# Feed-forward of block 1 by block matrices: seven block products in place of eight

## Chip, cores and metric

The kernel runs on one core of one Trainium2 chip. The metric is the device time of one execution in microseconds (us). The core has five engines that run their own programs in order and wait for each other by semaphores: TensorE (PE, the matmuls), VectorE (DVE), ScalarE (ACT), GpSimd (POOL) and SyncE (SP), which issues nearly all transfers (DMA) between memory and SBUF here. Matmul results land in PSUM.

## What is computed

Two transformer blocks run over 1024 tokens of width 1024, in fp32. Block 1 has a convolution branch, an attention branch, and a feed-forward part; block 2 has differential attention beside a short convolution, and a mixture of experts. The change concerns the feed-forward part of block 1 alone:

```python
D_FF = ((8 * D_MODEL // 3 + 255) // 256) * 256      # 2816
...
        x = x + merged @ w_out[l]
        h2 = rmsnorm(x, g_ffn[l])
        gu = h2 @ w_ffn_in[l]
        x = x + (jax.nn.silu(gu[..., :D_FF]) * gu[..., D_FF:]) @ w_ffn_out[l]
    return x
```

Block 2 begins with `modulate(rmsnorm_2(h, ...), sh1, sc1)`, where shift and scale come from `silu(c) @ w_ada`, a matrix of 1024 x 6144 that multiplies one row.

## The kernel before

Every fp32 operand of a product is split into a high part, rounded to the type that PE multiplies, and a low part, the rest: `split` (line 213) is one ACT operation (the cast) and one DVE operation (the difference). A product is then three: high by high, low by high, high by low (`mm3`, line 267); its matmuls have a 128x128 stationary block and a 128x512 moving one, and go into one PSUM bank of 128x512.

The tokens are two halves of 512. `b1_out` (line 732) multiplies by `w_out`, adds into the eight residual tiles `x1` (128 tokens x 1024) and, behind the last column block, calls `store` for each half. `store` calls `norm_T` (line 746): `row_inv` gives one over the root mean square per token (squares on ACT, a few small DVE steps), DVE scales copies `xn`, PE transposes them (`tpx`), and a split puts eight pairs of operands (128 channels x 512 tokens) into SBUF.

`ffn` (line 774) goes over 22 blocks `f` of 128 hidden channels. `gu(f)` loads and splits the gate and the up weights of the block (`w_gu`, 128x1024 each) and makes four products `pg`, `pu` (2 halves x gate and up, 24 matmuls each); ACT takes the silu, DVE multiplies by `pu` (line 792), and the result is split into operands. `down` (line 797) takes two blocks at a time, loads two blocks of `w_ffn_out`, and for each of 8 token tiles and 2 column halves makes a product `pd` of 6 matmuls (12 the last time), which DVE adds into `x1` (line 807). Between these blocks stand the steps of `ada` (line 835): it loads `w_ada` in 128x512 pieces, DVE multiplies each by a scalar per partition and sums up (lines 849 and 851), and PE sums over partitions with a matrix of ones (`pada`). `ada_end` (line 861) reads the result back, adds bias and gains. Behind the last `down` of each half, `b2_prep` (line 894) stores the residual to DRAM (`d_h`), normalises and transposes the half for block 2, whose first products are `pq` by `w2_k`.

The order of each engine's program is that of the code; tiles come from rotating pools (`bufs` tiles of a name), and a write to a reused tile waits for its last reader. SP issues loads in the order of the code too, which runs ahead of the products by what the pools hold. Here six rows of weights `wr` (128x1024) and four split ones fit, and PSUM has 3 banks for `mm` (`pg`, `pu`, `pw`), 2 for transposes and 3 for `pd`.

## Time and profile before

| what | value |
| --- | --- |
| time, median of 3 runs | 2835.47 us (2834.75 to 2836.74) |
| the profiled execution | 2836.5 us |
| its span in the trace | 2834.7 us, 1.8 us less |
| TensorE busy | 2704.4 us, 95% |
| VectorE busy | 2000.4 us, 71% |
| ScalarE busy | 1331.1 us, 47% |
| GpSimd busy | 187.3 us, 7% |
| mean granted TensorE clock | 0.98 |
| from the first `pg` to the first `pq` | 793.09 to 1529.91 us |

Durations come from one profiled execution. A busy share is a mean over the whole span, while each stage has its own limit, so the stretches are read one by one. An engine's idle time is put down to what released it ("<-ACT ych"). The duration of a matmul overlaps the next one's; the distance of their starts tells how fast they follow each other. The granted clock is TensorE's: 1.00 is 2.4 GHz, 0.50 is 1.2 GHz.

### The profile page before, as it was taken

Reading aid. Unit: us, or ns where it says so; the run is one execution under the profiler, and the core shown is the slowest. Engines: PE = TensorE matmul, PEld = TensorE weight load, DVE = VectorE, ACT = ScalarE, POOL = GpSimd, SP = SyncE. Lnnn points to the kernel's source line nnn. Section 1 sums busy time; section 2 is a strip of 40 time slices with the busy share of each in tenths; the row PEclk is TensorE's granted clock in tenths of the full one; section 3 lists DMA queues with packets and bytes.
Section 4 is the critical chain, followed back from the end, with each engine's and each line's share of the span. In section 5 each row is a group of like instructions: output and inputs, shape, how many; then the busy total and the mean of one; then the engine's idle time right before and its main releaser. Section 6 shows DMA issues by size and latency. Waiting matters only on the chain.

```text
span 2834.7 us, 39695 instructions
## 1 busy us (share of the span) xinstructions
PE 2704.4 (95%) x14546; PEld 2273.4 (80%) x14546; DVE 2000.4 (71%) x3679; ACT 1331.1 (47%) x2499; POOL 187.3 (7%) x273
## 2 busy tenths in 40 slices
PE   6999999989999999999999998999999599999995
PEld 5899777768988888888888987888887488888874
DVE  5998688745454665543326567898758799999987
ACT  4223467631131222111124455666433488888885
POOL 0000011000000000000000033100000100000101
PEclk9999999999999999999999999999999799999997
DMA  3124422054312343311113412221155899999986
GB/s 126 53 75 108 138 82 65 31 193 150 105 45 60 109 149 117 117 54 45 45 60 122 135 58 75 94 87 53 53 169 206 299 385 393 392 393 393 391 296 156
DMA packets 164594, 430.77 MB, mean 152 GB/s; under 512 B 36088, under 2 KB 47200, under 8 KB 164400
## 3 DMA queue, kind: packets, MB, share of 16 engines
q1 hardware_dynamic: 157328, 405.69, 40.3%
q0 software_dynamic: 7072, 22.55, 3.5%
q8 instruction: 114, 1.87, 0.3%
q14 instruction: 80, 0.66, 0.1%
HBM read 368.60 MB, written 59.57 MB: 151 GB/s over the span
## 4 chain that ended last, share of the span: by engine, by line
PE 87%; DVE 5%; DMA 3%; ACT 2%; issue 2%; POOL 0%; SPq 0%; POOLq 0%; ACTq 0%; DVEq 0%
PE pg L274 8%; PE pu L274 8%; PE pd L274 8%; PE pgate L274 7%; PE pw L274 6%; PE pnat L274 5%; PE pq L274 4%; PE pa L274 3%; PE po L1152 3%; PE peg L1508 2%; PE peu L1510 2%; PE peu L1509 2%; PE peg L1509 2%; PE peg L1510 2%; PE peu L1508 2%
## 5 line engine op out<-in xcount | busy, mean ns | idle before, releaser
L218 DVE TENSOR_TENSOR wl<-wr,wh 128x1024 fp32r<-128x1024 f32 (+1 forms) x248 | 298.8, 1226 | 186.7 <-ACT wh L217 184.7
L217 ACT CAST wh<-wr 128x1024 fp32r<-128x1024 f32 (+1 forms) x248 | 256.8, 1052 | 354.7 <-PE pd L274 159.7
L218 DVE TENSOR_TENSOR wl<-op,wh 128x1024 fp32r<-128x1024 f32 x285 | 334.5, 1220 | 17.7 <-ACT wh L217 15.9
L217 ACT CAST wh<-op 128x1024 fp32r<-128x1024 f32 x285 | 294.2, 1057 | 40.4 <-PE peg L1509 17.3
L274 PE MATMUL pd<-wh,op 128*128 128x512 f32 x704 | 187.6, 390 | 0.0
L274 PE MATMUL pgate<-op,wh 128*128 128x512 f32 x640 | 177.3, 406 | 3.8 <-ACT op L220 3.6
L807 DVE TENSOR_TENSOR x<-x,pd 128x512 f32<-128x512 f32 x160 | 108.3, 685 | 65.2 <-PE pd L274 65.1
L274 PEld LDWEIGHTS pd<-wh,op 128*128 128x128 f32 x704 | 131.8, 188 | 27.3 <-ACT wh L217 0.2
L369 DVE SCALAR_TENSOR_TENSOR c<-a,w_half,c 128x1019 f32<-128x1019 f32 (+28 forms) x120 | 148.0, 1263 | 0.4
L792 DVE TENSOR_TENSOR silu<-silu,pu 128x512 f32<-128x512 f32 x44 | 30.2, 687 | 159.5 <-PE pu L274 159.3
L274 PEld LDWEIGHTS pgate<-op,wh 128*128 128x128 f32 x640 | 118.4, 191 | 29.3 <-ACT op L220 8.2
L1131 ACT ACTIVATE ex<-ps,nmm 128x512 f32<-128x512 f32 (+1 forms) x192 | 116.9, 618 | 48.8 <-DVE nmm L1127 40.8
L274 PE MATMUL pq<-wh,op 128*128 128x256 f32 x768 | 114.8, 291 | 0.8 <-ACT wh L217 0.5
L851 DVE SCALAR_TENSOR_TENSOR acc<-wada,silu_c,acc 128x512 f32<-128x512 f32 x112 | 82.0, 749 | 41.5 <-DMA wada<-in_w_ada_dram 40.5
L1527 PE MATMUL ped<-wh,ehh 128*128 128x512 f32 x256 | 103.4, 404 | 7.2 <-ACT wh L217 7.2
L274 PE MATMUL pw<-wh,op 128*128 128x256 f32 (+1 forms) x640 | 109.2, 307 | 0.0
L274 PE MATMUL pd<-wl,op 128*128 128x512 f32 x352 | 106.6, 390 | 0.0
L274 PEld LDWEIGHTS pq<-wh,op 128*128 128x128 f32 x768 | 103.4, 196 | 3.8 <-ACT wh L217 1.4
L1508 PE MATMUL peg<-wh,xsh 128*128 128x512 f32 x256 | 101.7, 397 | 0.4 <-ACT xsh L217 0.3
L1510 PE MATMUL peg<-wl,xsh 128*128 128x512 f32 x256 | 101.0, 395 | 0.9 <-DVE wl L218 0.9
L1510 PE MATMUL peu<-wl,xsh 128*128 128x512 f32 x256 | 101.7, 397 | 0.0
L1529 PE MATMUL ped<-wl,ehh 128*128 128x512 f32 x256 | 99.5, 395 | 2.2 <-DVE wl L218 2.1
(469 smaller groups left out, 6570.9 us busy)
## 6 DMA issues: line engine op xcount, KB each, us to landing
op<-in_w_down_dram SPq DMA_DIRECT2D x96, 512.0 KB, 7.5
op<-in_w_up_dram SPq DMA_DIRECT2D x95, 512.0 KB, 6.3
op<-in_w_gate_dram SPq DMA_DIRECT2D x94, 512.0 KB
wada<-in_w_ada_dram SPq DMA_DIRECT2D x96, 256.0 KB, 2.7
wr<-in_w_gu_dram SPq DMA_DIRECT2D x44, 512.0 KB, 3.6
wr<-in_w_gate_dram SPq DMA_DIRECT2D x34, 512.0 KB
wr<-in_w_up_dram SPq DMA_DIRECT2D x33, 512.0 KB, 6.0
wr<-in_w_down_dram SPq DMA_DIRECT2D x32, 512.0 KB, 8.4
```

The costliest lines, as they stand in the source:

```text
L217: nc.scalar.copy(hi, src)
L218: nc.vector.tensor_sub(lo, src, hi.bitcast(F32))
L274: r = nc.tensor.matmul(ps, a[k], b[k], start=first and s == 0 and k == 0, stop=last and s == 2 and k == n - 1)
L369: nc.vector.scalar_tensor_tensor(c[:, s:], a[:, :S - s], wh[:, j * 31 + 30 - s:j * 31 + 31 - s], c[:, s:], op0=OP.mult, op1=OP.add)
L807: v.tensor_add(xs[tt][:, sl], xs[tt][:, sl], p)
L1131: nc.scalar.activation(ex[:, sl], p, AF.Exp, bias=nmm, accum_out=z[:, m * 3 + pi:m * 3 + pi + 1])
L1152: nc.tensor.matmul(po[:, :256], part[:, j * 128:(j + 1) * 128], V[j0 + j], start=j0 + j == 0 and part is ah, stop=j0 + j == 9 and part is al)
L1508: nc.tensor.matmul(p, xh[:, ks], wh[:, ws], start=k == 0, stop=False)
L1509: nc.tensor.matmul(p, xl[:, ks], wh[:, ws], start=False, stop=False)
L1510: nc.tensor.matmul(p, xh[:, ks], wl[:, ws], start=False, stop=k == KD - 1)
L1527: nc.tensor.matmul(pd[half], a[:, fs], wh[:, ws], start=f == 0, stop=False)
L1529: nc.tensor.matmul(pd[half], a[:, fs], wl[:, ws], start=False, stop=f == KD - 1)
```

## The change

The feed-forward's matrices are taken as 2 x 2 blocks, and a product of such matrices is made from seven products of sums and differences of blocks (Winograd's form) in place of eight.

**Up.** The normalised tokens' operand has the blocks half 0 and half 1 by channels 0 to 511 and 512 to 1023. `ffn_norm` stores the residual `x1` to DRAM (`d_x1`) and scales the tiles in place. For half 0 it transposes and splits into B[1] and B[2]; for half 1 `ffn_sums` transposes, scales on ACT, and makes the five operands B[6], B[5], B[7], B[3], B[4] from sums of both halves: 33 operations on DVE (13 sums, 20 differences of splits) and 11 on POOL (`t3`, `t2`). `ffn_up(j)` makes, for j = 0 to 10, seven products for gate and up (m = 0, 1) of 128x512 weight blocks: 7 x 2 x 12 matmuls into 6 PSUM banks. Weight sums `sc` (s1, s2) are made by DVE, `s3` and s4 by POOL; each weight or sum is split into one tile `ws` (of 7). DVE adds the products together from PSUM (`plus`), ACT and DVE gate them, and the seven combinations needed later are stored to DRAM as `d_a{j}`, five of them made by POOL. `ada` becomes a generator, of which two steps stand behind each product for j of 1 and more.

**Down.** After all of it, pools are closed and opened again, `x1` is loaded back from `d_x1`, `ada_end` runs, and `ffn_down` makes seven products, 3, 5, 4, 1, 7, 6, 2. Each has 11 steps: load `ar` (a stored combination) and one or two blocks `br` of `w_ffn_out` (128x512 each), combine these into `bc` (DVE, or POOL in products 7 and 6), split both, and 12 matmuls into four PSUM banks. Then the four banks are added to (or taken from) one or two quarters of `x1`. `b2_prep` runs for half 0 behind product 7, for half 1 behind product 2.

The diff, cut where `...` stands (among it the old body of `ffn`, which stands above):

```diff
--- before.py
+++ after.py
...
@@ -771,55 +772,208 @@
...
-    def ffn(self, xs, xh, xl, then):
+    def ffn_norm(self, xs, half, g):
+        grp = xs[4 * half:4 * half + 4]
+        for tt in range(4 * half, 4 * half + 4):
+            self.nc.sync.dma_start(self.d_x1[tt], xs[tt])
+        inv = self.row_inv(grp)
+        for i, t in enumerate(grp):
+            self.nc.vector.tensor_scalar(t, t, inv[:, i:i + 1], None, op0=OP.mult)
+        if half == 0:
+            hi, lo = self.ops(0)
+            self.to_T(grp, hi, lo, g)
+            self.B = {1: (hi[:4], lo[:4]), 2: (hi[4:], lo[4:])}
+        else:
+            self.ffn_sums(grp, g)
+    def ffn_sums(self, grp, g):
+        nc = self.nc
+        v = nc.vector
+        (b11h, b11l), (b21h, b21l) = self.B[1], self.B[2]
+        new = {n: [self.op(1) if n in (5, 6) else self.page_of(self.pt) for _ in range(4)] for n in (6, 5, 7, 3, 4)}
+        fs = []
+        for k in range(4):
+            f = self.pg(name="x1", pool=self.px)
+            for kk in range(2):
+                tp = self.tp(name="tpx")
+                for i, t in enumerate(grp):
+                    nc.tensor.transpose(tp[:, i * 128:(i + 1) * 128], t[:, (k + 4 * kk) * 128:(k + 4 * kk + 1) * 128], self.ident)
+                nc.scalar.activation(f[:, kk * 512:(kk + 1) * 512], tp, AF.Copy, scale=g[:, k + 4 * kk:k + 4 * kk + 1])
+            fa, fb = f[:, :512], f[:, 512:]
+            t3 = self.hp(name="t3")
+            (nc.gpsimd if k else v).tensor_sub(t3, fb, fa)
+            v.tensor_sub(fa, fa, b11l[k].bitcast(F32))
+            v.tensor_sub(fa, fa, b11h[k].bitcast(F32))
+            t2 = self.hp(name="t2")
+            v.tensor_sub(t2, fb, fa)
+            self.split(t2, *new[6][k])
+            self.split(t3, *new[7][k])
+            fs.append((fa, fb, t2))
+        for k in range(4):
+            self.split(fs[k][0], *new[5][k])
+            nc.gpsimd.tensor_sub(fs[k][2], b21h[k].bitcast(F32), fs[k][2])
+            nc.gpsimd.tensor_add(fs[k][2], fs[k][2], b21l[k].bitcast(F32))
+        for k in range(4):
+            self.split(fs[k][1], *new[3][k])
+        for k in range(4):
+            self.split(fs[k][2], *new[4][k])
+        for n, o in new.items():
+            self.B[n] = [hi for hi, lo in o], [lo for hi, lo in o]
...
+    def wsplit(self, src):
+        t = self.wp.tile([128, 1024], F32R, name="ws", tag="ws", bufs=self.ws)
+        self.split(src, t[:, :512], t[:, 512:])
+        return t
+    def wk(self, src):
+        t = self.wsplit(src)
+        return [t[:, k * 128:(k + 1) * 128] for k in range(4)], [t[:, 512 + k * 128:640 + k * 128] for k in range(4)]
+    def ffn_up(self, j, ada):
         nc = self.nc
         v = nc.vector
         A = self.A
...
+        B = self.B
+        f0, f1 = [], []
+        for fs, f in ((f0, 2 * j), (f1, 2 * j + 1)):
+            for m in range(2):
+                r = self.wp.tile([128, 1024], F32, name="wr", tag="wr", bufs=4)
+                nc.sync.dma_start(r, A["w_gu"][2 * f + m])
+                fs.append(r)
+        L, R = slice(0, 512), slice(512, 1024)
+        def product(n, w):
+            ps = [self.mm(name=f"p{m}") for m in range(2)]
+            for m in range(2):
+                self.mm3(ps[m], w(m), B[n])
+            ada(2)
+            return ps
+        def tiles():
+            return [self.hp(name=n) for n in ("hg", "hu")]
+        def plus(out, x, ps):
+            for m in range(2):
+                v.tensor_add(out[m], x[m], ps[m])
+        def gate(x):
+            nc.scalar.activation(x[0], x[0], AF.Silu)
+            v.tensor_mul(x[0], x[0], x[1])
+        p = product(1, lambda m: self.wk(f0[m][:, L]))
+        u = tiles()
+        for m in range(2):
+            nc.scalar.copy(u[m], p[m])
+        p = product(2, lambda m: self.wk(f0[m][:, R]))
+        c11 = tiles()
+        plus(c11, u, p)
+        gate(c11)
+        s1, s2, s3, s4 = [], [], [], []
+        for m in range(2):
+            t = self.hp(name="sc")
+            v.tensor_add(t, f1[m][:, L], f1[m][:, R])
+            s1.append(self.wk(t))
+            v.tensor_sub(t, t, f0[m][:, L])
+            s2.append(self.wk(t))
+            s4.append(t)
+        p = product(6, lambda m: s2[m])
+        plus(u, u, p)
+        for m in range(2):
+            t = self.hp(name="s3")
+            nc.gpsimd.tensor_sub(t, f0[m][:, L], f1[m][:, L])
+            s3.append(t)
+        p = product(7, lambda m: self.wk(s3[m]))
+        c21 = tiles()
+        plus(c21, u, p)
+        p = product(5, lambda m: s1[m])
+        c22 = tiles()
+        plus(c22, c21, p)
+        plus(u, u, p)
+        gate(c22)
+        for m in range(2):
+            nc.gpsimd.tensor_sub(s4[m], f0[m][:, R], s4[m])
+        p = product(3, lambda m: self.wk(s4[m]))
+        plus(u, u, p)
+        gate(u)
+        p = product(4, lambda m: self.wk(f1[m][:, R]))
+        plus(c21, c21, p)
+        gate(c21)
+        c11, c12, c21, c22 = c11[0], u[0], c21[0], c22[0]
+        a11, a21, a12, a22 = c11, c12, c21, c22
+        d = self.dram.tile([8, 128, 512], F32, name=f"d_a{j}")
+        self.d_a.append(d)
+        def out(n, t):
+            nc.sync.dma_start(d[n], t)
+        def both(n, op, x, y, dst=None):
+            t = self.hp(name="hc") if dst is None else dst
+            op(t, x, y)
+            out(n, t)
+        out(3, a11)
+        out(4, a22)
+        both(1, nc.gpsimd.tensor_add, a11, a22)
+        both(2, nc.gpsimd.tensor_add, a21, a22)
+        both(6, nc.gpsimd.tensor_sub, a21, a11, a21)
+        both(5, nc.gpsimd.tensor_add, a11, a12)
+        both(7, nc.gpsimd.tensor_sub, a12, a22, a12)
+    def ffn_down(self, xs, then):
+        nc = self.nc
+        v = nc.vector
+        W = self.A["w_ffn_out"]
+        L, R = slice(0, 512), slice(512, 1024)
+        add, sub = v.tensor_add, v.tensor_sub
+        for n, b, c in ((3, ((0, R), (1, R), sub), ((0, R, add), (1, R, add))),
+                        (5, ((1, R),), ((0, L, sub), (0, R, add))),
+                        (4, ((1, L), (0, L), sub), ((0, L, add), (1, L, add))),
+                        (1, ((0, L), (1, R), add), ((0, L, add), (1, R, add))),
+                        (7, ((1, L), (1, R), nc.gpsimd.tensor_add), ((0, L, add),)),
+                        (6, ((0, L), (0, R), nc.gpsimd.tensor_add), ((1, R, add),)),
+                        (2, ((0, L),), ((1, L, add), (1, R, sub)))):
+            ps = [self.mm(name="pd") for _ in range(4)]
+            for j in range(DFF // 256):
+                t = self.hp(name="ar")
+                nc.sync.dma_start(t, self.d_a[j][n])
+                x = self.wsplit(t)
+                r = []
+                for o, cols in b[:2]:
+                    t = self.hp(name="br", bufs=6)
+                    nc.sync.dma_start(t, W[2 * j + o][:, cols])
+                    r.append(t)
+                if len(b) == 3:
+                    t = self.hp(name="bc")
+                    b[2](t, r[0], r[1])
+                else:
+                    t = r[0]
+                y = self.wsplit(t)
+                for i in range(4):
+                    q = slice(i * 128, (i + 1) * 128), slice(512 + i * 128, 640 + i * 128)
+                    self.mm3(ps[i], ([x[:, q[0]]], [x[:, q[1]]]), ([y[:, L]], [y[:, R]]), first=j == 0, last=j == DFF // 256 - 1)
+            for i in range(4):
+                for h, cols, op in c:
+                    t = xs[4 * h + i]
+                    op(t[:, cols], t[:, cols], ps[i])
+            if n == 7:
+                then(0)
+        then(1)
     def ada_setup(self):
...
@@ -849,12 +1004,12 @@
                         v.tensor_scalar(acc, w, s, None, op0=OP.mult)
                     else:
                         v.scalar_tensor_tensor(acc, w, s, acc, op0=OP.mult, op1=OP.add)
+                    yield
             for (r, cc), acc in zip(outs, accs):
...
                 nc.sync.dma_start(self.d_mod[r:r + 1, half * 512:(half + 1) * 512], acc[0:1])
...
@@ -1620,36 +1775,54 @@
         gates.finish()
         p.release()
         self.weights(2, 4)
-        self.psum(3, 2, 3)
+        self.psum(6, 2, 0)
         p = self.phase("pD")
         mh, ml = self.b1_merge()
         p.release()
-        px = self.phase("px1")
+        self.pt = self.open("pT", "right")
+        self.px = self.phase("px1")
         xs = self.b1_load_x()
-        pt = self.open("pT", "right")
         p = self.phase("pE")
...
         g = self.cload("g_ffn", [128, KD])
-        xh, xl = [], []
...
-        self.b1_out(mh, ml, xs, store)
+        self.d_x1 = self.dram.tile([NT, 128, D], F32, name="d_x1")
+        self.b1_out(mh, ml, xs, lambda half: self.ffn_norm(xs, half, g))
+        p.release()
+        self.px.release()
+        self.wp.release()
+        self.wp = self.open("wp", "left")
+        self.ws = 7
+        self.d_a = []
+        p = self.phase("pU")
+        for n, k in (("acc", 2), ("wada", 2), ("hc", 2), ("s3", 2), ("hg", 5), ("sc", 2), ("hu", 4)):
+            for _ in range(k):
+                self.hp(name=n)
         self.ada_setup()
-        self.ffn(xs, xh, xl, lambda half: None if x2_only else self.b2_prep(xs, half))
...
+        ada = Paced(self.ada())
+        for j in range(DFF // 256):
+            self.ffn_up(j, ada if j else lambda n: None)
+        ada.finish()
         p.release()
-        pt.release()
+        self.pt.release()
+        self.wp.release()
+        self.wp = self.open("wp", "left")
+        self.ws = 8
+        px = self.phase("px2")
+        xs = []
+        for tt in range(NT):
+            t = self.pg(name="x1")
+            self.nc.sync.dma_start(t, self.d_x1[tt])
+            xs.append(t)
+        p = self.phase("pV")
+        self.ada_end()
+        self.ffn_down(xs, lambda half: self.b2_prep(xs, half))
+        p.release()
         px.release()
+        self.wp.release()
+        self.wp = None
+        self.weights(2, 4)
+        self.psum(3, 2, 3)
...
```

DVE's program at the start of the feed-forward, before. `xn` are scaled tokens of half 1, `op0` its operands; `silu` and `op1` are the first gate's result and operands:

```order
L757 TENSOR_SCALAR xn_8174<-x1_7028,inv_row_8090 128x256
L757 TENSOR_SCALAR xn_8176<-x1_7030,inv_row_8090 128x256
L221 SCALAR_TENSOR_TENSOR op0_8066<-tpx_8158,c_g_ffn_7040,op0_8066 128x512
L221 SCALAR_TENSOR_TENSOR op0_8067<-tpx_8165,c_g_ffn_7040,op0_8067 128x512
L757 TENSOR_SCALAR xn_8178<-x1_7032,inv_row_8090 128x256
L792 TENSOR_TENSOR silu_8265<-silu_8265,pu_8240 128x512
L221 SCALAR_TENSOR_TENSOR op0_8068<-tpx_8180,c_g_ffn_7040,op0_8068 128x512
L221 SCALAR_TENSOR_TENSOR op0_8069<-tpx_8187,c_g_ffn_7040,op0_8069 128x512
L218 TENSOR_TENSOR op1_8268<-silu_8265,op1_8268 128x512
```

And after, where `f0` and `op1` are low parts of the summed operands, `ones` belongs to `ada_setup`, and `ws` is a split weight of the first steps:

```order
L219 TENSOR_TENSOR op1_8084<-x1_8166,op1_8084 128x512
L219 TENSOR_TENSOR f0_8092<-x1_8166,f0_8092 128x512
L219 TENSOR_TENSOR f0_8093<-t2_8114,f0_8093 128x512
L219 TENSOR_TENSOR f0_8094<-t2_8137,f0_8094 128x512
L219 TENSOR_TENSOR f0_8095<-t2_8160,f0_8095 128x512
L219 TENSOR_TENSOR f0_8096<-t2_8183,f0_8096 128x512
L209 MEMSET ones_f_8255 128x128
L210 CAST ones_8254<-ones_f_8255 128x128
L219 TENSOR_TENSOR ws_8268<-wr_8258,ws_8268 128x512
L219 TENSOR_TENSOR ws_8283<-wr_8260,ws_8283 128x512
L219 TENSOR_TENSOR ws_8304<-wr_8258,ws_8304 128x512
```

The normalisation of half 1 stood among the first products' work; now all of the sums stand ahead of the first split weight.

SP's program at the border from the last gate and up to the last projection back, before (`wr` is a weight's tile), as far as the loads for block 2 and the first store of the residual:

```order
L233 DMA wr_12569<-in_w_gu_dram 128x1024
L233 DMA wr_12575<-in_w_gu_dram 128x1024
L233 DMA wr_12693<-in_w_ffn_out_dram 128x1024
L233 DMA wr_12699<-in_w_ffn_out_dram 128x1024
L233 DMA wr_12705<-in_w_ffn_out_dram 128x1024
L233 DMA wr_12711<-in_w_ffn_out_dram 128x1024
L233 DMA wr_13264<-in_w2_k_dram 128x1024
L233 DMA wr_13270<-in_w2_k_dram 128x1024
L901 DMA d_h_12829<-x1_7018 128x1024
L901 DMA d_h_12829<-x1_7020 128x1024
```

And after, from the last stores of the combinations on (`hg` and `hc` hold them; `modt` is the first load of `ada_end`, and seven more such small ones follow it, then the first `ar`):

```order
L920 DMA d_a10_11918<-hg_11674 128x512
L1815 DMA x1_11943<-d_x1_7044 128x1024
L1815 DMA x1_11945<-d_x1_7044 128x1024
L920 DMA d_a10_11918<-hc_11929 128x512
L920 DMA d_a10_11918<-hg_11806 128x512
L1815 DMA x1_11947<-d_x1_7044 128x1024
L1815 DMA x1_11949<-d_x1_7044 128x1024
L1815 DMA x1_11951<-d_x1_7044 128x1024
L1815 DMA x1_11953<-d_x1_7044 128x1024
L1815 DMA x1_11955<-d_x1_7044 128x1024
L1815 DMA x1_11957<-d_x1_7044 128x1024
L1025 DMA modt_11962<-d_mod_8253 64x128
```

Loads of `w_ffn_out` stood among those of `w_gu`; now the stores of the last step and the whole reload of `x1` come first.

SP's program at the end of the feed-forward, after, where before the two `w2_k` loads stood ahead of the first `d_h` store (the last rows of the fence of before):

```order
L954 DMA ar_14097<-d_a10_11918 128x512
L1056 DMA d_h_13426<-x1_11951 128x1024
L1056 DMA d_h_13426<-x1_11953 128x1024
L1056 DMA d_h_13426<-x1_11955 128x1024
L1056 DMA d_h_13426<-x1_11957 128x1024
L234 DMA wr_14304<-in_w2_k_dram 128x1024
L234 DMA wr_14310<-in_w2_k_dram 128x1024
L234 DMA wr_14438<-in_w2_q_dram 128x1024
```

The stores of half 1's residual now stand ahead of the first weights of block 2.

## Rows read from the trace of the kernel before

**Rows 1.** The page, part 1 (busy us, share, instructions) and part 4 (chain).

```profile
PE 2704.4 (95%) x14546; PEld 2273.4 (80%) x14546; DVE 2000.4 (71%) x3679; ACT 1331.1 (47%) x2499; POOL 187.3 (7%) x273
...
PE 87%; DVE 5%; DMA 3%; ACT 2%; issue 2%; POOL 0%; SPq 0%; POOLq 0%; ACTq 0%; DVEq 0%
```

**Rows 2.** Windows: length, busy us of PE, PEld, DVE, ACT, POOL; PE clock, DMA share, GB/s.

```profile
1000.00:1100.00 100.00, 100.00 (x442) 82.42 (x441) 60.50 (x86) 16.61 (x23) 0.00 (x0) 1.00 0.43 132
```

**Rows 3.** Timeline of PE: start us, us, line, operation, count [idle before]; three stretches.

```profile
792.13 1.12 PE L274 MATMUL pw<-wl,op 128*128 128x256 f32 x8
793.09 2.00 PE L274 MATMUL pg<-f,wh 128*128 128x512 f32 x8
...
1003.05 1.07 PE L274 MATMUL pd<-wh,op 128*128 128x512 f32 x4
1003.96 0.62 PE L274 MATMUL pd<-wl,op 128*128 128x512 f32 x2
1004.41 1.07 PE L274 MATMUL pd<-wh,op 128*128 128x512 f32 x4
...
1529.00 1.07 PE L274 MATMUL pd<-wl,op 128*128 128x512 f32 x4
1529.91 2.57 PE L274 MATMUL pq<-wh,op 128*128 128x256 f32 x19
```

**Rows 4.** Groups of PE's instructions, 740 to 1620 us: count | busy us, mean ns | idle.

```profile
L274 PE MATMUL pd<-wh,op 128*128 128x512 f32 x704 | 187.6, 390 | 0.0
L274 PE MATMUL pd<-wl,op 128*128 128x512 f32 x352 | 106.6, 390 | 0.0
```

**Rows 5.** Waits of DVE, 740 to 1620 us: us in total, times, longest.

```profile
DVE silu L792 <- PE pu L274: 159.3, 33, 8.3
...
DVE acc L851 <- DMA wada<-in_w_ada_dram: 37.6, 32, 3.6
```

**Rows 6.** Timeline of DVE: the norm of half 0, from last addition to reciprocal root.

```profile
777.31 0.42 DVE L741 TENSOR_TENSOR x<-x,pw 128x256 f32<-128x256 f32 x1 [2.46 <-PE pw L274]
...
781.17 0.16 DVE L263 SCALAR_TENSOR_TENSOR inv_row<-rs_t,rs_i 128x4 f32<-128x4 f32 x1
```

**Rows 7.** Timeline of DVE, and its group of in-place scalings (busy, mean ns | idle).

```profile
1000.38 1.28 DVE L807 TENSOR_TENSOR x<-x,pd 128x512 f32<-128x512 f32 x2
...
L322 DVE TENSOR_SCALAR x<-x,inv_row 128x1024 f32<-128x1024 f32 x8 | 5.5, 749 | 0.1
```

**Rows 8.** Timeline of DVE and POOL at three places of block 2.

```profile
1658.08 1.81 DVE L1142 SCALAR_TENSOR_TENSOR ex<-ex,cf,ex 128x512 f32<-128x512 f32 x3
...
1668.26 3.12 DVE L1142 SCALAR_TENSOR_TENSOR ex<-ex,cf,ex 128x512 f32<-128x512 f32 x3
1669.49 1.60 POOL L989 TENSOR_TENSOR fp<-fp,rot 128x512 f32<-128x512 f32 x1
...
1759.32 3.76 DVE L250 TENSOR_SCALAR rs_i<-ms 128x4 int32<-128x4 int32 x1
1759.33 2.51 POOL L988 TENSOR_TENSOR fp<-fp,rope 128x512 f32<-128x512 f32 x2
1761.80 1.25 POOL L989 TENSOR_TENSOR fp<-fp,rot 128x512 f32<-128x512 f32 x1
```

**Rows 9.** Timeline of PE where block 1 turns from gates to merging.

```profile
601.34 0.80 PE L274 MATMUL py<-ych,wh 128*128 128x512 f32 x1 [6.74 <-ACT ych L220]
```

**Rows 10.** Windows with the columns of rows 2: that border, and the experts' stage.

```profile
600.00:605.00 5.00, 2.15 (x4) 0.94 (x4) 3.14 (x5) 3.30 (x6) 0.00 (x0) 0.50 0.83 285
605.00:610.00 5.00, 4.68 (x14) 3.20 (x13) 3.87 (x6) 2.99 (x5) 0.00 (x0) 0.72 0.83 239
2430.00:2440.00 10.00, 10.00 (x52) 8.34 (x51) 10.00 (x11) 8.55 (x12) 0.56 (x1) 1.00 1.03 420
```

**Rows 11.** The page, part 6, with groups below it: DMA issues, KB, us to landing.

```profile
ta<-d_gate SPq DMA_DIRECT2D x16, 256.0 KB, 2.9
...
d_h<-x SPq DMA_DIRECT2D x8, 512.0 KB, 2.6
```

More of the change, by code (lines that the diff above doesn't have):

```diff
@@ L798, in down @@
-        def down(fs, last=False):
-            ws = [self.weight(A["w_ffn_out"][f]) for f in fs]
-            for tt in range(NT):
-                q = slice((tt % 4) * 128, (tt % 4 + 1) * 128)
-                for c in range(2):
-                    p = self.at(name="pd")
-                    sl = slice(c * 512, (c + 1) * 512)
-                    self.mm3(p, ([hs[f][0][tt // 4][:, q] for f in fs], [hs[f][1][tt // 4][:, q] for f in fs]),
-                             ([w[0][:, sl] for w in ws], [w[1][:, sl] for w in ws]))
-                    v.tensor_add(xs[tt][:, sl], xs[tt][:, sl], p)
-                if last and tt % 4 == 3:
-                    then(tt // 4)
-            for f in fs:
-                del hs[f]
@@ L832, in ada_setup, with ada @@
         self.ones = self.constr(1.0, "ones")
-    def ada(self, step):
+    def ada(self):
         nc = self.nc
         v = nc.vector
-        for half in range(2):
-            j = 2 * step + half
+        for j in range(12):
+            step, half = j // 2, j % 2
             outs = [(step, 0)] + ([(6 + step, 1)] if step < 2 else [])
@@ L1600, in moe, with block1 @@
             nc.gpsimd.indirect_dma_start(out=out, out_offset=at, in_=fr, in_offset=None)
[L1603 removed]
+    def block1(self):
         p = self.phase("pA")
```

56 lines of the change are left out of this document (10 added, 46 removed).

## The prediction

> **What bounds the kernel now.** I read the page first: TensorE (PE) is busy 95% of the span, and the chain of work that ended last is PE for 87% of its length [rows 1]. VectorE (DVE) is busy 71% and GpSimd (POOL) hardly at all, but these are averages over very different stages. So the next view is the stretches inside the feed-forward (FFN): in the 100 us from 1000 on PE is busy for all 100, at a granted clock of 1.00, with 442 recorded matmuls, DVE for 60.5 us, POOL not at all, and the DMA engines move 132 GB/s [rows 2]. In this stage nothing but the number of matmuls sets the time, and whatever takes matmuls away there is worth its full price until DVE, or a wait at a border, comes due.
>
> The timeline gives the price of one: from 1003.05 to 1004.41 us six matmuls start, so one 128x512 takes 1.36 / 6 = 0.2267 us [rows 3]. (The duration printed for a single one, 0.39 us, overlaps the next.) The product `pd` has 704 + 352 = 1056 of them [rows 4]; `pg` and `pu` have the same number, 22 column blocks x 2 halves x 24. Together 3168, or 718.2 us. The FFN stretches from the first `pg` at 793.09 to the first `pq` of block 2 at 1529.91 [rows 3]: 736.8 us. The other 18.6 us are the 32 matmuls of `ada` (7.3 us at the same price), and 64 transposes and short waits (11.3 us). PE enters and leaves this stretch without a gap: `pg` starts within a microsecond of the last `pw`, `pq` within one of the last `pd`. DVE in it mostly waits for PE (159.3 us for `pu` alone), and for the weights of `ada` 37.6 us [rows 5].
>
> **What goes.** Seven block products instead of eight: up has 11 x 168 = 1848 matmuls, down 7 x 11 x 12 = 924, 2772 in all against 3168. 396 x 0.2267 = **-89.8 us**. All of it lies on the path. Everything else that the change does costs time or is hidden.
>
> **Start gap.** Before, the first gate and up products need half 0 alone, and the normalisation of half 1 runs beside them. Now DVE's program has all 33 instructions that build the five summed operands ahead of the first weight split `ws` (the first place in the order), and no product can start without that split. PE stands idle for this chain. From the last `pw`, about 793 us, the old trace gives its parts. For half 0, from the last addition at 777.31 to the end of the reciprocal root at 781.33, the norm took 4.0 us [rows 6]; with about 0.7 for PE's last result and the squares still open, an estimate, that is 4.7 us. Four in-place scalings of 0.749 us [rows 7] overlap the first transposes; with those, and ScalarE (ACT) copying PSUM out, DVE can start on the sums at about 9.4 us. A two-input 128x512 operation takes 1.28 / 2, about 0.605 us from one start to the next [rows 7], so 33 take 20.0 us. In their midst stand 11 POOL operations at 1.25 us [rows 8], some of which have to be waited for, in order (8 x 1.25, half of it beside DVE: some 4 us). To this come the two for `ones`, and one split: 9.4 + 20 + 4 + 0.6 = **34 us**. Bounds: 28 (POOL wholly hidden, transposes early) and 42 (POOL wholly in line).
>
> **Up.** 1848 matmuls are 418.9 us, the 32 of `ada` 7.3. What must be weighed is DVE. Each of the 11 steps takes PE 168 x 0.2267 + 0.7 = 38.8 us. DVE has 540 instructions in the stage, and with the small ones of `ada` 51.7 a step: 51.7 x 0.605 = 31.3 us. By itself that fits. But nine POOL operations a step, 9 x 1.25 = 11.3 us, run beside it, and the old trace shows what this does. Three DVE operations `ex` took 1.81 us alone and 3.12 us where POOL's 128x512 ran beside them; and a DVE operation on 4 columns took 3.76 us while POOL ran 2.51 and then 1.25 us, thus until POOL was through [rows 8]. So a POOL operation holds up a DVE operation on SBUF for its whole duration. The 14 additions a step that read PSUM, some 27% of DVE's work, I take as not held up, so POOL costs DVE about 8 of its 11.3 us. Waits for the weights of `ada`, 37.6 / 11 = 3.4 us a step before [rows 5], now have more slack; I keep 2. DVE then needs 31.3 + 8 + 2 = 41.3 us against 38.8: 2.5 a step, 25 us over ten steps, if nothing absorbed it. The splits of weights run ahead of the products by a pool of seven tiles, about 6.7 us, and where PE waits, POOL too has slack. I take a stall of **12 us**, and as bounds 2 (POOL falls in DVE's idle time) and 58 (below).
>
> The Trainium skill, "SBUF — State Buffer", section "SBUF: two separate sides", says that a GpSimd operation and a DVE operation with two SBUF inputs take an exclusive lock for the whole instruction, and the loser blocks. The 3.76 us row agrees for an operation with one input, which that sentence covers only in a two-port mode.
>
> **Border up to down.** Before there is none: loads of `w_ffn_out` stand among those of `w_gu`, prefetched (second place in the order). Now SP has the last stores of `d_a10`, two of which wait for POOL's results after the last product, and behind these six loads of `x1` (512 KB), eight small ones for the modulation, and only then the first `ar` and `br`. After PE's last product: gate on ACT and DVE 1.7 us, two POOL operations 2.7 more (4.4), six loads of 0.5 MB at 420 GB/s [rows 10] 7.5 us and 2.6 us until one has landed [rows 11], with the later issues waiting for the landing of a transfer eight earlier: some 16 us. Then the first `ar`/`br` land 2.9 us after issue [rows 11], and the combination, the split on ACT and PE follow: **20.7 us**. The nearest row for such a change of phase is at 601.34 us, where PE waited 6.74 us for the splits of a freshly loaded operand [rows 9]. Bounds 12 (the loads don't hold up the small ones) and 26.
>
> **Down.** 924 x 0.2267 = 209.5, and 4.5 us for the transposes of block 2's norm, half of what stood in the FFN before. DVE has 77 steps of two splits, a combination in three products, and 48 additions: about 141 us by the same price, under PE's 209. The loads are the question: a step of 2.72 us brings 768 KB in five of seven products, 289 GB/s. Loads of 256 KB and 512 KB in 2 KB and 4 KB rows ran at 285 GB/s at 600 us, those of 512 KB at 420 at 2430 us [rows 10]. Stall **4 us**, between 0 and 31 (rival 3).
>
> **Clock.** After the wait at 601 us the granted clock was 0.50, the level of 1.2 GHz, for 5 us and 0.72 in the next five [rows 10]. Matmuls at half speed for that long lose 2 to 3 us; two long waits: **4 us**.
>
> **End.** Before, the first weights of block 2 (`w2_k`) are loaded ahead of the stores of `d_h`, and `pq` starts behind the last `pd` at once [rows 3]. Now four stores that wait for the last additions into `x1` stand ahead of them (third place). Eight additions of 0.605 us, a load (512 KB, near the 2.6 us of a store [rows 11]) and the split on ACT and DVE, some 8 us; the chain of half 1's norm, on which PE waits anyway afterwards, takes part of it back: **+5.7 us**, bounds 2 and 10.
>
> **The sum.** After: 34 + (418.9 + 7.3 + 12) + 20.7 + (209.5 + 4.5 + 4) + 4 = 714.9, and 5.7 at the end: 720.6 us, against 736.8. The difference is -16.2 us. The profiled execution took 2836.5 us (its span is 2834.7), 1 us above the median of the three runs, so 2820.3 by it, 2819.3 by the median: I forecast **2820**.
>
> **Rivals.** (1) Slower: *POOL's port binds the up stage.* If all of POOL's 11.3 us fall on DVE, a step costs it 31.3 + 11.3 + 2 = 44.6 against 39.5 with `ada`: 5.1 x 11 = 56 us, less the lead of 6.7: 50, or 38 more than the forecast, **2858**; without the lead, and without `ada` in step 0, 58: 2866. The change breaks even where the stall reaches 28 us, some 2.5 a step. For it: the 3.76 us row; against: additions from PSUM, and POOL's operations come bunched after the last product of a step. (2) Faster: *the gaps are short.* Start 28, border 12, a stall of 2, loads without any: 6 + 8.7 + 10 + 4 less, **2792**. For it: both chains are my sums of parts, and DVE has 39.5 us of 100 free in the old FFN [rows 2]; against: the order of DVE's and SP's programs. (3) *Down waits for its loads.* At 239 GB/s, the rate at 605 us [rows 10], 768 KB take 3.29 us; 55 steps x 0.57 = 31 us, 27 more than the forecast: **2847**. (4) It does not do what it says, or the clock stays low in the up stage because PE waits so often: at 0.72 of the pace for 100 us, +39. The order shows 2772 matmuls, so only the second is real.
>
> The Trainium skill, "DMA: Bandwidth & Descriptors", section "Bandwidth", asks for 1 MiB or more in a transfer for three quarters of the peak; these have 256 KB. No row here isolates that size; by that rule rival 3 would come true, and its price stands above.
>
> **Chances.** Forecast 0.47 (2806 to 2838), rival 1 0.25, rival 2 0.18, rival 3 0.07, rival 4 0.03. A measurement of this kernel tells about 0.2%, 5.7 us, from no change: 2829.8 and 2841.2. Faster: most of the forecast's case and all of rival 2, 0.56. Same: the forecast's upper edge and the lower edges of rivals 1 and 3, 0.15. Slower: 0.29. The range from 2795 to 2864 leaves out the far ends of rivals 1, 2 and 4.
>
> **What would show it.** PE's count in the FFN 2772 at 0.227 us apart; an idle PE of 28 to 42 us before the first product, ended by a split `ws`; DVE busy over 90% in the up stage, its splits longer than 0.69 us beside POOL (mean over 0.75), and PE's idle time there ended by `ws` splits; one idle stretch of 12 to 26 us ended by the split of `ar` or `bc`; in down a DMA rate near 289 GB/s without idle PE. The forecast is wrong if DVE in up is under 85% busy and PE still waits (then it is the order), or if down's PE waits for DMA.

## The result and the profile after

The changed kernel takes **2859.65 us** (median of 4 runs, 2857.16 to 2861.55), the kernel before 2836.1 in the same session: a ratio of 1.0081, with a 95% interval from 1.0064 to 1.0099. It is 23.5 us slower. The forecast was 16 us faster, 2820; the time lies inside the range, but on the wrong side, and almost on rival 1's number.

The page of the profile after, parts 1 and 4, beside [rows 1]:

```profile
PE 2638.7 (92%) x14150; PEld 2215.1 (78%) x14150; DVE 2254.6 (79%) x3997; ACT 1437.2 (50%) x2739; POOL 398.7 (14%) x405
...
PE 78%; DVE 11%; DMA 4%; issue 3%; ACT 3%; POOL 1%; SPq 0%; POOLq 0%; ACTq 0%; DVEq 0%
```

PE has 396 instructions fewer, so the seven products are there. But its share of the chain fell from 87% to 78%, and DVE's rose from 5% to 11%. The timeline of PE shows where it now waits (columns as in [rows 3]):

```profile
787.96 0.96 PE L275 MATMUL pw<-wl,op 128*128 128x256 f32 x6
794.37 2.58 PE L803 MATMUL tpx<-ident,x 128*128 128x128 f32 x8 [5.45 <-DVE x L782]
...
827.51 2.08 PE L275 MATMUL p<-op,ws 128*128 128x512 f32 x4 [23.47 <-ACT ws L218]
833.66 6.60 PE L275 MATMUL p<-op,ws 128*128 128x512 f32 x20 [4.07 <-DVE ws L219]
...
1000.92 3.02 PE L275 MATMUL p<-op,ws 128*128 128x512 f32 x12 [1.09 <-ACT ws L218]
...
1085.78 1.19 PE L275 MATMUL p<-op,ws 128*128 128x512 f32 x4 [1.40 <-ACT ws L218]
1087.62 2.14 PE L275 MATMUL p<-op,ws 128*128 128x512 f32 x8 [0.65 <-DVE ws L219]
1091.78 4.62 PE L275 MATMUL p<-op,ws 128*128 128x512 f32 x12 [2.02 <-ACT ws L218]
...
1223.34 4.52 PE L275 MATMUL p<-op,ws 128*128 128x512 f32 x12 [3.13 <-ACT ws L218]
...
1283.70 4.92 PE L275 MATMUL p<-f,ws 128*128 128x512 f32 x21
1305.74 0.34 PE L1037 MATMUL pmod<-ident,modt 64*128 64x64 f32 x1 [17.12 <-DVE modt L1033]
1309.85 10.35 PE L275 MATMUL pd<-ws 128*128 128x512 f32 x33 [3.77 <-ACT ws L218]
...
1477.28 1.09 PE L764 MATMUL tpx<-ident,xn 128*128 128x128 f32 x4 [4.50 <-DVE xn L758]
...
1499.27 37.65 PE L275 MATMUL pd<-ws 128*128 128x512 f32 x164
1543.80 3.19 PE L764 MATMUL tpx<-ident,xn 128*128 128x128 f32 x12 [6.87 <-DVE xn L758]
...
1562.37 3.09 PE L275 MATMUL pq<-wh,op 128*128 128x256 f32 x16
```

To compare the ends, a mark behind the disturbance is needed: the first `psw` of block 2 (groups of that tile, first and last start behind the durations; the kernel after, then before):

```profile
L1408 PE MATMUL psw<-wr,shb x16: 179/262/283, 1615.3 to 1623.0; 128*128 128x16 f32 x16
```

```profile
L1253 PE MATMUL psw<-wr,shb x16: 181/262/283, 1592.2 to 1599.9; 128*128 128x16 f32 x16
```

From the end of the last `pw` (793.2 before, 788.9 after) to there, before took 799 us and after 826.4:

| stretch, us | before | forecast | after |
| --- | --- | --- | --- |
| last `pw` to first product | 0 | 34 | 38.6 |
| up, first product to last | 736.8 with the two below | 438.2 | 461.1 |
| border | 0 | 20.7 | 21.2 |
| down, with the 4 for the clock | in the 736.8 | 222 | 227.1 |
| last `pd` to first `psw` | 62.3 | 68.0 | 78.4 |
| sum | 799 | 783 | 826.4 |

The sum is 27.4 us longer than before, the time only 23.5, since the last `pw` ended 4.3 us earlier. That point wanders between 788.9 and 795.0 us among kernels that are alike up to there, so I give the change no credit for it, and read single times to some us only; the stretches are steadier. The first was 38.6 us in nine kernels; among the kernels below that are alike in a stretch, up lies between 458.0 and 461.6 us, down between 222.3 and 227.6, the end between 78.3 and 80.0.

Two lines show the up stage from DVE's side (groups as in [rows 4], 827 to 1289 us): the accumulation of `ada`, one operand of which is multiplied by a scalar, and an addition with one operand in PSUM.

```profile
L1006 DVE SCALAR_TENSOR_TENSOR acc<-wada,silu_c,acc 128x512 f32<-128x512 f32 x112 | 106.1, 957 | 14.6 <-DMA wada<-in_w_ada_dram 14.2
L869 DVE TENSOR_TENSOR hu<-hu,p 128x512 f32<-128x512 f32 x77 | 51.5, 679 | 14.4 <-PE p L275 14.2
...
L888 DVE TENSOR_TENSOR sc<-sc,wr 128x512 f32<-128x512 f32 x22 | 22.6, 1027 | 0.3
```

The first took 749 ns before the change, the last kind 0.69 us where nothing disturbs it. The addition from PSUM is as long as ever.

### The profile page after: what moved, and what is told of

It reads as the page before. It is cut to its first block, busy times and chain, and to the rows that moved or that the text cites. A ratio compares the mean times of both kernels' runs of the same rounds, so it can differ in the third digit from the quotient of the medians.

```text
span 2857.0 us, 40521 instructions
## 1 busy us (share of the span) xinstructions
PE 2638.7 (92%) x14150; PEld 2215.1 (78%) x14150; DVE 2254.6 (79%) x3997; ACT 1437.2 (50%) x2739; POOL 398.7 (14%) x405
## 4 chain that ended last, share of the span: by engine, by line
PE 78%; DVE 11%; DMA 4%; issue 3%; ACT 3%; POOL 1%; SPq 0%; POOLq 0%; ACTq 0%; DVEq 0%
PE p L275 9%; PE pgate L275 7%; PE pd L275 7%; PE pw L275 6%; PE pnat L275 5%; PE pq L275 5%; PE pa L275 3%; PE po L1307 3%; PE peg L1663 2%; PE peu L1665 2%; PE peg L1664 2%; PE peu L1664 2%; PE peg L1665 2%; PE peu L1663 2%; PE ped L1682 2%
## 5 line engine op out<-in xcount | busy, mean ns | idle before, releaser
L275 PE MATMUL p<-op,ws 128*128 128x512 f32 x1056 | 256.0, 400 | 45.2 <-ACT ws L218 39.8
L219 DVE TENSOR_TENSOR wl<-wr,wh 128x1024 fp32r<-128x1024 f32 (+1 forms) x182 | 217.6, 1221 | 100.4 <-ACT wh L218 96.6
L275 PEld LDWEIGHTS p<-op,ws 128*128 128x128 f32 x1056 | 203.0, 193 | 94.0 <-ACT ws L218 44.0
L218 ACT CAST wh<-wr 128x1024 fp32r<-128x1024 f32 (+1 forms) x182 | 188.5, 1054 | 111.1 <-PE pw L275 37.1
L275 PE MATMUL pd<-ws 128*128 128x512 f32 x924 | 217.6, 397 | 3.8 <-ACT ws L218 3.8
L275 PEld LDWEIGHTS pd<-ws 128*128 128x128 f32 x924 | 176.6, 192 | 40.7 <-ACT ws L218 4.0
L275 PE MATMUL p<-f,ws 128*128 128x512 f32 x792 | 183.6, 389 | 0.0
L275 PEld LDWEIGHTS p<-f,ws 128*128 128x128 f32 x792 | 149.1, 188 | 31.1
L1006 DVE SCALAR_TENSOR_TENSOR acc<-wada,silu_c,acc 128x512 f32<-128x512 f32 x112 | 106.1, 957 | 14.6 <-DMA wada<-in_w_ada_dram 14.2
```

The source lines that it names most:

```text
L218: nc.scalar.copy(hi, src)
L219: nc.vector.tensor_sub(lo, src, hi.bitcast(F32))
L275: r = nc.tensor.matmul(ps, a[k], b[k], start=first and s == 0 and k == 0, stop=last and s == 2 and k == n - 1)
L1006: v.scalar_tensor_tensor(acc, w, s, acc, op0=OP.mult, op1=OP.add)
```

## Experiments

Theory after the result: the up stage waits because POOL's operations hold up DVE. Rivals: DVE's own load, the places where these operations stand, the order of other engines. In the table, all times are us, and "first" is the stretch from the last `pw` to the first product that uses `ws`; in "two products first" and the three kernels "all" it holds products 1 and 2 of step 0, 10.9 us that are then missing from "up".

| kernel | time | first | up | border | down | end |
| --- | --- | --- | --- | --- | --- | --- |
| changed | 2859.65 | 38.6 | 461.1 | 21.2 | 227.1 | 78.4 |
| no POOL | 2839.1 | 38.6 | 434.2 | 21.7 | 226.5 | 80.0 |
| POOL's to DVE | 2838.0 | 38.6 | 435.7 | 22.6 | 226.3 | 78.4 |
| no `ada` | 2841.6 | 38.6 | 438.5 | 22.5 | 227.6 | 78.3 |
| combinations to DVE | 2842.6 | 38.6 | 446.7 | 21.4 | 222.3 | 79.9 |
| sums to DVE | 2850.9 | 38.6 | 450.8 | 21.4 | 226.2 | 79.3 |
| late reload | 2856.4 | 38.6 | 458.0 | 13.9 | 231.4 | 79.8 |
| two products first | 2853.5 | 49.7 | 443.6 | 21.8 | 224.7 | 79.4 |
| one PSUM | 2860.4 | 38.6 | 461.6 | 20.9 | 226.3 | 76.7 |
| PSUM and weights | 2856.5 | 38.6 | 461.5 | 21.2 | 228.5 | 71.1 |
| all | 2813.7 | 42.2 | 421.7 | 14.1 | 230.2 | 72.1 |
| all, sums on POOL | 2817.8 | 47.6 | 421.4 | 13.8 | 230.6 | 71.8 |
| all, down's too | 2808.3 | 42.3 | 421.4 | 13.3 | 223.1 | 72.3 |

The changed kernel and the three "all" have the median of four runs, the others a single run each. The kernel before took 2835.2 to 2836.9 beside them.

### POOL's nine operations a step left out

```diff
-            nc.gpsimd.tensor_sub(t, f0[m][:, L], f1[m][:, L])
-            s3.append(t)
+            s3.append(f0[m][:, L])
...
-        p = product(3, lambda m: self.wk(s4[m]))
+        p = product(3, lambda m: self.wk(f0[m][:, R]))
...
+        for n, t in ((1, a11), (2, a21), (6, a21), (5, a12), (7, a12)):
+            out(n, t)
```

> Leaves out the nine POOL operations of each step of the up stage: the two weight sums s3 and the two s4 are replaced by the plain weight blocks, and the five combinations are stored uncombined (the values are then others; all matmuls, splits, stores and loads remain). In the changed kernel the up stage lasts 461.1 us, 34.9 more than its matmuls (426.2). Theory (POOL's operations hold up DVE's): DVE's operations on SBUF were longer than alone by about 60 us in the stage, so this goes; the stage ends within 426 to 440 us, the time is 20 to 35 us shorter (2825 to 2840), and acc falls from 957 to about 750 ns. Rival (the waits come from DVE's own load and the order of ACT's program, POOL is beside the point): the stage stays above 450 us and the time within 8 us of 2859.7.

The stage fell to 434.2 us, the time by 20.5. `acc` is back at 747 ns. The windows from 950 to 1250 us (columns as in [rows 2]) of this kernel, and of the changed one below, give DVE's need:

```profile
950.00:1250.00 300.00, 298.35 (x1317) 246.64 (x1316) 246.12 (x391) 104.29 (x182) 0.00 (x0) 1.00 0.51 168
```

```profile
950.00:1250.00 300.00, 282.31 (x1203) 229.04 (x1202) 272.08 (x363) 94.03 (x168) 104.64 (x63) 0.98 0.49 161
```

A step has 168 matmuls beside those of `ada`, and of the counts of these windows 28 and 26 are `ada`'s; they are left out here and below. Without POOL DVE is busy 246.12 us while PE makes the other 1289, 32.1 us for 168; with POOL 272.08 for 1177, 38.8. So nine POOL operations cost DVE 6.8 us a step, and with them its need is as long as the 38.8 us that a step takes PE.

### The same nine given to DVE

```diff
-            nc.gpsimd.tensor_sub(t, f0[m][:, L], f1[m][:, L])
+            v.tensor_sub(t, f0[m][:, L], f1[m][:, L])
...
-        both(1, nc.gpsimd.tensor_add, a11, a22)
+        both(1, v.tensor_add, a11, a22)
```

(and so for s4 and the other four combinations)

> Gives the same nine operations of each step to DVE: nothing left out. Theory (a POOL operation costs DVE as much as it takes itself): 9 x 0.6 = 5.4 us a step more for DVE, about 5.4 a step less hold-up; the up stage stays within 8 us of 461 and the time within 8 us of 2859.7. Rival (POOL's operations run beside DVE's nearly for nothing): 11 x 5.4 = 60 us more for DVE, of which most becomes waiting of PE: 2890 to 2920.

Neither came: the stage got 25 us shorter, with 99 operations more on DVE. Its window and its groups:

```profile
950.00:1250.00 300.00, 297.57 (x1309) 244.83 (x1308) 281.97 (x459) 105.05 (x182) 0.00 (x0) 1.00 0.52 166
```

```profile
L1006 DVE SCALAR_TENSOR_TENSOR acc<-wada,silu_c,acc 128x512 f32<-128x512 f32 x112 | 82.0, 745 | 8.7 <-DMA wada<-in_w_ada_dram 8.4
...
L924 DVE TENSOR_TENSOR hc<-hg 128x512 f32<-128x512 f32 x33 | 22.5, 683 | 0.1
```

281.97 for 1281 is 37.0 us for 168: the nine cost DVE 4.9 us when it makes them itself, 6.8 when POOL does. DVE is busy 94% here, and PE waits 2.4 of 300 us; with a need of 38.8 us it waited 17.7. The Trainium skill, "SBUF — State Buffer", section "SBUF: two separate sides", has a POOL operation and a DVE operation with two inputs in SBUF exclude each other for a whole instruction. The trace agrees: `acc` has two and took 957 ns for 745, the addition with one input in PSUM 679. And this pair of runs shows the consequence: DVE loses more by POOL's help than it would by doing the work.

### `ada` left out

```diff
-                    else:
-                        v.scalar_tensor_tensor(acc, w, s, acc, op0=OP.mult, op1=OP.add)
```

> Leaves out the 112 accumulating operations of ada (all but the first piece of each sum; loads, the splits and PE's two matmuls remain), so DVE has 106 us less in the up stage; POOL's work remains. Theory (DVE is short of time only because all three come together: its own work, ada and POOL's hold-ups): DVE's need falls from 37 to about 28 us a step against 38.8, the waits in the up stage end but for the first one, stage 430 to 442 us, time 2828 to 2842. Rival (POOL's port alone makes the stall, at the places where its operations stand): the stage stays above 450 us.

438.5 us: with POOL's operations in place, but some 9 us a step less for DVE (223.94 us busy for 1274 matmuls from 950 to 1250, 29.5 us for 168), the later waits are all but gone. POOL's hold-ups alone do not make the stall; they do so on top of a DVE that is nearly full.

### Half of the nine at a time

The five combinations to DVE, the sums left on POOL; then the other way round (the same edits as above, in part).

> Of the changed kernel's nine POOL operations a step, the five combinations alone go to DVE; the four sums s3, s4 stay on POOL. With all nine on DVE the up stage went from 461.1 to 435.7 us. Theory (the combinations, which follow each other at the border of two steps just when the next step's first sums and splits are due, make the waits): most of the gain is here, stage 436 to 443 us. Rival (each of the nine counts alike): 5/9 of it, 445 to 450 us.

> The counterpart: the four sums s3, s4 go to DVE, the five combinations stay on POOL. Theory (the combinations at the border make the waits): stage 452 to 462 us. Rival (each counts alike): 4/9 of 25 us, 447 to 452 us. If it is the one with the larger gain, the waits come from POOL's answer being waited for (s3 and s4 feed splits of the same step, the combinations feed only stores).

446.7 and 450.8 us. By 5/9 and 4/9 of the 25.4 us of all nine it would be 447.0 and 449.8, so within the spread of this stage each counts alike, and my theory that the bunch at the border of two steps does the harm falls. DVE's need per 168 matmuls is 37.6 and 38.4 us in these two (277.40 us for 1240, 277.28 for 1214), and PE's wait in the 300 us, 8.1 and 10.4 us, stands in the same order as with 37.0 (2.4) and 38.8 (17.7): the stall rises steeply in the last 2 us before DVE's need is that of PE.

### The reload of `x1` behind down's first product

```diff
+            if n == 3:
+                for tt in range(NT):
+                    nc.sync.dma_start(xs[tt], self.d_x1[tt])
+                self.ada_end()
...
-            self.nc.sync.dma_start(t, self.d_x1[tt])
...
-        self.ada_end()
```

> The reload of x1 and all of ada_end stand behind the eleven steps of down's first product, ahead of its additions; nothing else. Theory (the border is the queue of loads ahead of the first ar and br): PE's idle time there falls from 21.2 us to 8 to 12 us, the time by about 10 to 13 (2846 to 2850), with no new wait at the additions, since product 3 lasts 30 us. Rival (the border is the chain gate, POOL, store, load of d_a10): it stays above 16 us and the time within 5 of 2859.7.

In part: PE's timeline at the border and at the end of the first product.

```profile
1300.69 33.13 PE L275 MATMUL pd<-ws 128*128 128x512 f32 x132 [13.91 <-ACT ws L218]
1335.50 0.24 PE L1041 MATMUL pmod<-ident,modt 64*128 64x64 f32 x1 [1.68 <-DVE modt L1037]
1335.67 1.20 PE L275 MATMUL pd<-ws 128*128 128x512 f32 x4
1337.93 2.50 PE L275 MATMUL pd<-ws 128*128 128x512 f32 x5 [1.06 <-DVE ws L219]
```

The border shrank by 7.3 us, so the queue of loads was at least a third of it, and the 8 to 12 us that the theory expected to be left were 13.9. The rest stayed, four of the eight loads of `x1` still stood ahead of the first `ar`, and 4.3 us came back in down, where `ada_end` and the additions now stood ahead of the next product's splits.

### Products 1 and 2 of step 0 first

```diff
+        for m in range(2):
+            for n in (1, 2):
+                p = self.first[n, m] = self.mm(name="pf")
+                ...
+                self.mm3(p, (h, l), self.B[n])
...
-        p = product(1, lambda m: self.wk(f0[m][:, L]))
+        p = product(1, lambda m: self.wk(f0[m][:, L])) if j else [self.first[1, m] for m in range(2)]
```

> Products 1 and 2 of step 0, which need half 0 alone, are made with the old weight tiles (48 matmuls, 10.9 us) and stand ahead of the last sums of half 1; nothing left out. Theory (PE's 38.6 us before the first product are a chain on DVE that no load or weight shortens): these 10.9 us fall into the gap, the next product starts 38 to 42 us after the last pw, the time falls by 8 to 13 us. Rival (the gap is the arrival or the splits of the weights): the next product moves with the products, and the time stays within 4 us of 2859.7.

```profile
805.94 1.09 PE L276 MATMUL pf<-op,wh 128*128 128x512 f32 x4
839.71 4.34 PE L276 MATMUL p<-op,ws 128*128 128x512 f32 x12 [32.67 <-ACT ws L219]
```

The 10.9 us of matmuls fell into the gap, but the next product moved 11.1 us back: it is product 6, which needs two more sums and splits on DVE for each of gate and up, and these stand behind all of the sums of half 1 again. What was gained, 7.2 us from the last `pw` to `psw`, is mostly the stumble after the first product (under the start gap below). So the gap is DVE's chain, as the theory has it, but its 38 to 42 us for the next product were 49.7: work for PE does not shorten the gap as long as DVE's order stays.

### The end: PSUM's pool and the weights

```diff
-            ps = [self.mm(name="pd") for _ in range(4)]
+            ps = [(self.at if i % 2 else self.mm)(name="pd") for i in range(4)]
```

(and `self.psum(3, 2, 3)` ahead of down instead of behind it; in the second kernel also `self.weights(2, 4)`, with a pool of its own for `ws`)

> PSUM's pool is opened in block 2's layout (3, 2, 3 banks) ahead of down and not again behind it; pd takes two banks of each kind; the loads stay as they are. From the last pd to the first psw the changed kernel takes 78.4 us, the kernel before 62.2 from its first pq. Theory (the pool that is opened anew keeps pq behind all of half 1's transposes in PE's program): pq runs between the transposes again, but only once its weights, loaded behind the stores of d_h, are split: 5 to 9 us less at the end. Rival (the weights alone delay pq): nothing changes there, 76 to 80 us.

> As the kernel with one PSUM pool, and block 2's pool of weights is opened ahead of down, so that w2_k is loaded and split before the last product (the tiles ws of down go from 8 to 6 for it). Theory (both stand in the way of pq): the end falls from 78.4 to 62 to 66 us, the time by 12 to 16. Rival (the loads are not late): as with one PSUM pool alone, to within 2 us.

76.7 and 71.1 us from 78.4. With one PSUM pool alone `pq` does run between half 1's transposes, once its weights are split, but little came of it:

```profile
1549.90 1.65 PE L275 MATMUL pq<-wh,op 128*128 128x256 f32 x6 [0.48 <-ACT wh L218]
1551.34 1.05 PE L764 MATMUL tpx<-ident,xn 128*128 128x128 f32 x4
```

In the second kernel `pq` follows `pd` without a gap:

```profile
1537.71 2.66 PE L275 MATMUL pd<-ws 128*128 128x512 f32 x11
1540.21 2.08 PE L275 MATMUL pq<-wh,op 128*128 128x256 f32 x16
```

So the pool by itself was worth little, and both together 7.3 us, where 12 to 16 were expected; early weights by themselves were not tried, so how the 7.3 us divide is open. And 71.1 is still 8.8 more than the 62.3 of before: a later `pq` waits 4.34 us for ACT's copy `fp`, and half 1's transposes still wait, five of them 0.8 to 2.1 us. What holds these was not tried.

### All at once

All of the above that helped, and four changes more: the sums of half 1 wholly on DVE, the reload of `x1` spread over down's first product, `ada_end` behind its second, and half 0's norm for block 2 three steps into product 6.

> All that is left of the gaps at once, nothing left out: POOL's operations of the up stage and of the sums on DVE, products 1 and 2 of step 0 ahead, the reload of x1 spread over down's first product and ada_end behind its second, one PSUM pool and early w2_k, half 0's norm for block 2 three steps into product 6. By the theories: up -25 us, sums -3 to +5, start -10, border -8 to -12, end -12 to -16, half 0's norm -3 to -5: 2791 to 2808, faster than the kernel before by 1.0 to 1.6%. Rival (the gains overlap, since DVE at 94% in up has no slack and the gaps return elsewhere): 2815 to 2830.

2813.69 us (2811.93 to 2815.37), a ratio to the kernel before of 0.9919 (0.9903 to 0.9936): 0.8% faster than the kernel before and 1.6% faster than the changed one. That is less than expected, for the border (14.1), down (230.2) and the end (72.1) kept more than the theories allowed.

> As the combined kernel, with the 11 operations in the sums of half 1 back on POOL. In the combined kernel the next product after products 1 and 2 of step 0 begins 42.2 us after the last pw. Theory (POOL holds DVE up for longer than DVE itself would take): 44 to 50 us, the time 2 to 8 us longer than 2813.7. Rival (POOL works beside DVE's 33 operations): 36 to 40 us, the time 2 to 6 us shorter.

2817.79 us: the first stretch is 47.6 against 42.2 us. Eleven operations on POOL cost 5.4 us more there than on DVE.

> As the combined kernel, and down's 22 combinations bc of products 7 and 6 on DVE too. Theory (a POOL operation costs DVE its own length of 1.25 us and more, one on DVE 0.6): DVE gets no fuller there, PE did not wait in these products before: within 3 us of 2813.7. Rival (DVE becomes the bound of products 7 and 6): 5 to 15 us more.

**2808.33 us** (2804.61 to 2810.15), ratio 0.9898 (0.9882 to 0.9915): where no more than 3 us either way were expected from the last 22 POOL operations, in down, the time fell by 5.4, and down went from 230.2 to 223.1. By the starts of the matmuls 5.2 of these 7 us are in product 6 (41.6 to 36.4), beside which half 0's norm stands in these two kernels, in PE's waits for it and at a low clock behind them. The first two products, which the edit does not touch, were 3.2 us shorter as well, so the split of the 7 us is not sure. This is the fastest kernel of the case, 1.0% below the kernel before.

## Why the prediction was wrong, step by step

- **What goes**, -89.8 us: right. 396 instructions fewer, and PE at 0.227 us a matmul wherever it runs at full clock (222 recorded in 50 us, those at its edges included).
- **Start gap**: mechanism right, but the 38.6 us for 34 flatter the sum. The first four matmuls use the high part of `ws` alone, which ACT's cast makes. The split on DVE, with which my sum ended, came later: PE waited 4.07 us more and went on at 833.66, 44.7 us behind the last `pw`, outside the bounds of 28 to 42. DVE began the sums after 9.2 us, for 9.4, but took 34.5 us for them (the first three rows), where I had 20 + 4; the term for POOL was mis-sized. POOL's operations lasted 1.6 us there, not 1.25, and DVE's beside them 1.75 (the other four):

```profile
798.08 0.69 DVE L807 TENSOR_TENSOR t<-x 128x512 f32<-128x512 f32 x1 [1.86 <-ACT x L804]
...
830.12 2.48 DVE L219 TENSOR_TENSOR f<-t,f 128x512 fp32r<-128x512 f32 x4
...
832.92 2.49 DVE L219 TENSOR_TENSOR ws<-wr,ws 128x512 fp32r<-128x512 f32 x4
```

```profile
812.52 0.69 DVE L811 TENSOR_TENSOR t<-x 128x512 f32<-128x512 f32 x1
813.12 1.75 DVE L808 TENSOR_TENSOR x<-x,op 128x512 f32<-128x512 f32 x1
814.80 1.75 DVE L219 TENSOR_TENSOR f<-t,f 128x512 fp32r<-128x512 f32 x1
816.47 0.68 DVE L219 TENSOR_TENSOR op<-t,op 128x512 fp32r<-128x512 f32 x1
```

- **Up**: here the forecast's sign was lost: the stall is 34.9 us where I took 12. DVE's own work was 32.1 us a step for 31.3 forecast, the hold-ups 6.8 for my 8, and the waits for the weights of `ada` 14.2 us in ten steps for my 2 a step. With these my sum gives 40.2 us against 38.8, 14 us over ten steps, so the prices were right or a little too high. What failed is the sentence that the lead of seven `ws` tiles absorbs half: from step 4 on PE waited 17.7 us. The rest of the 34.9 are 7.1 at the first product (72 matmuls took 23.4 us from 827.5 on, for 16.3), which belong to the start's chain, and some 8 of matmuls at a low clock behind the four longest waits (1.87 to 3.99 us), which I counted nowhere in this stage; some 2 lie at the edges of the waits. Behind the seven waits of 0.65 to 1.40 us the clock stayed up: twelve matmuls took 3.02 us at 1000.92 and 4.52 at 1223.34.

  All eleven waits from step 4 on stand ahead of the matmuls of product 6. For these DVE makes and splits s1 and s2 in turn, though s1's splits are for product 5, and by the trace were done at least 13 us before PE used them. The last of these waits, with POOL busy beside it from 1216.34 to 1221.36:

```profile
1216.78 3.46 DVE L1006 SCALAR_TENSOR_TENSOR acc<-wada,silu_c,acc 128x512 f32<-128x512 f32 x2
1220.16 1.74 DVE L219 TENSOR_TENSOR ws<-sc,ws 128x512 fp32r<-128x512 f32 x1
1221.94 0.69 DVE L888 TENSOR_TENSOR sc<-sc,wr 128x512 f32<-128x512 f32 x1
```

  So a DVE that is nearly full makes PE wait first at the place with the shortest lead. Whether s2 ahead of s1 would have spared these waits was not tried.

  The granted clock (the last column but two; below 1.00 it is a mix of the levels of 2.4 and 1.2 GHz) in windows where PE waited, and in one, the second, where it did not:

```profile
825.00:870.00 45.00, 38.41 (x156) 31.11 (x157) 44.61 (x63) 15.76 (x26) 12.81 (x8) 0.86 0.36 113
950.00:990.00 40.00, 40.00 (x178) 33.11 (x177) 38.51 (x51) 13.48 (x24) 15.09 (x10) 1.00 0.42 140
1070.00:1110.00 40.00, 35.91 (x148) 28.29 (x147) 34.39 (x50) 11.43 (x20) 10.19 (x7) 0.96 0.64 197
1190.00:1230.00 40.00, 35.00 (x140) 28.01 (x139) 35.16 (x46) 10.38 (x19) 15.16 (x9) 0.91 0.52 168
```

- **Border**: 21.2 for 20.7, and right in its parts: SP issued the first `ar` 15.3 us behind PE's last matmul, for some 16, and five of the small loads ahead of it waited 4.3 us for loads of `x1` (SP's waits, 1286 to 1306 us: us in total, times, longest). The late reload bore out the queue of loads as a good third.

```profile
SPq L1031 <- DMA x<-d_x: 4.3, 5, 1.1
...
1303.90 0.35 SPq L954 DMA_DIRECT2D ar<-d_a  x1
```

- **Down**: no wait for loads; PE was busy for all of 1350 to 1400 us at 273 GB/s, so rival 3 was wrong. In place of the 4 us of stall stand 6.5 of waits for half 0's norm (4.50 and 1.96 us), which I had taken as free, and the low clock behind the border and in product 6 cost some 6.5 us for 4, by the starts of the matmuls: together the 5 us over.
- **End**: +16.1 for +5.7. I had read SP's order and not PE's. There, `pq` stood behind all of half 1's transposes, and with one PSUM pool between them; with that and early weights 7.3 us came back. The remaining 8.8 are not explained.
- **Rivals**: rival 1's time, 2858, was nearly hit, but not by its price: it had POOL cost 50 us of stall, and its sum counts `ada` twice (39.5 us a step for PE, where 38.8 has it already); with 38.8 it gives 57 us and 2865. Taking POOL out of the stage gave 27 us; the start, down and the end gave the rest, so the hit was luck. Of rival 4, a low clock in up for 39 us, some 8 came true.
